# Layer normalisation, 16,384 rows of 1,024 floats: larger tiles in the in-place ring, new first tiles, and a second load queue at the start

## The chip, the cores and the metric

One core of one Trainium2 chip. The metric is the device time of one execution in microseconds (us), the median of several runs. The profile's span is about 2 us shorter than that time. All runs used here are at a granted clock of 1.0.

## The reference

```python
def reference(x, eps):            # x: (32, 512, 1024) float32
    mean = np.mean(x, axis=-1, keepdims=True)
    var = np.var(x, axis=-1, keepdims=True)
    return ((x - mean) / np.sqrt(var + eps)).astype(np.float32)
```

Each of 16,384 rows is normalised by itself. 67.1 MB are read, 67.1 MB written.

## The kernel before

A tile is K rows on each of the 128 partitions, K x 4 KB per partition. It is loaded into a ring of 48 rows per partition, normalised in place and stored from there. A slot is loaded again only after its store has landed.

```python
TILES = (2, 2, 4) + (8,) * 14 + (4, 2, 2)
RING = 48
GROUP = 8
# ...
    def rows_of(a, row, K):       # K rows of a partition lie together in HBM
        return a[row * P : (row + K) * P].rearrange("(p k) d -> p k d", p=P)
# ...
    def group(xs, G):              # its body in words
        # VectorE: 2 bn_stats per row (128x512 each)
        # GpSimd: nine small operations from the statistics to the sum of squares
        # ScalarE: sqrt; VectorE: reciprocal; GpSimd: -mean * rstd
        # ScalarE: one Identity activation per row, in place
# ...
        for K, row, pos in place(TILES, RING):
            nc.sync.dma_start(out=ring[:, pos : pos + K, :], in_=rows_of(x2, row, K))
            for g in range(0, K, GROUP):
                G = min(GROUP, K - g)
                group(ring[:, pos + g : pos + g + G, :], G)
            nc.scalar.dma_start(out=rows_of(o2, row, K), in_=ring[:, pos : pos + K, :])
```

## Time and profile before

| | before |
|---|---|
| time | 318.12 us (318.04 to 318.23, 3 runs) |
| span of the profiled run | 316.1 us |
| VectorE, ScalarE, GpSimd busy | 50%, 49%, 14% |
| load queue q1, store queue q10: share of the DMA engines' time | 49.6%, 49.3% |
| first packet, last packet ends | 1.76 us, 314.91 us |

The trace lists every DMA packet with start, duration and size. From that list I work out the *shortfall* at a time t: t less what the bytes moved by t would take at 435.2 GB/s (the ceiling that the prediction cites). It is the DMA time lost so far, averaged over the 16 engines, and it shows where it is lost.

### The profile page before, as it was taken

Reading aid. Unit: us, or ns where it says so; the run is one execution under the profiler, and the core shown is the slowest. Engines: PE = TensorE matmul, PEld = TensorE weight load, DVE = VectorE, ACT = ScalarE, POOL = GpSimd, SP = SyncE. Lnnn points to the kernel's source line nnn. Section 1 sums busy time; section 2 is a strip of 40 time slices with the busy share of each in tenths; the row PEclk is TensorE's granted clock in tenths of the full one; section 3 lists DMA queues with packets and bytes.
Section 4 is the critical chain, followed back from the end, with each engine's and each line's share of the span. In section 5 each row is a group of like instructions: output and inputs, shape, how many; then the busy total and the mean of one; then the engine's idle time right before and its main releaser. Section 6 shows DMA issues by size and latency. Waiting matters only on the chain.

```text
span 316.1 us, 794 instructions
## 1 busy us (share of the span) xinstructions
DVE 157.1 (50%) x277; ACT 154.3 (49%) x149; POOL 45.1 (14%) x204
## 2 busy tenths in 40 slices
DVE  2368596547092561916529074190652908363030
ACT  1336296692833809247091561900651956196321
POOL 0420202201102020020200202002020020221120
DMA  7999999999999999999999999999999999999996
GB/s 301 433 399 469 431 416 425 433 427 444 420 448 419 444 419 444 435 427 444 419 448 415 448 424 440 423 448 419 444 423 440 423 435 429 446 428 417 455 411 282
DMA packets 5766, 134.27 MB, mean 425 GB/s; under 512 B 640, under 2 KB 640, under 8 KB 640
## 3 DMA queue, kind: packets, MB, share of 16 engines
q1 hardware_dynamic: 2880, 67.11, 49.6%
q10 hardware_dynamic: 2880, 67.11, 49.3%
q14 instruction: 6, 0.05, 0.0%
HBM read 67.11 MB, written 67.11 MB: 425 GB/s over the span
## 4 chain that ended last, share of the span: by engine, by line
DMA 58%; DVE 17%; ACT 9%; POOL 6%; issue 3%; another core or an unknown queue 3%; ACTq 0%; POOLq 0%; DVEq 0%; SPq 0%
DMA ring<-in_x_dram 32%; DMA out_dram<-ring 27%; DVE stats L75 17%; ACT ring L111 8%; POOL half L64 1%; ACT std L103 1%; POOL dev L97 1%; POOL nmean L87 1%; POOL dev L100 1%; POOL dev L90 1%; POOL dev L96 1%; POOL nmean L67 1%; POOL ss L67 1%; DVE rstd L107 0%
## 5 line engine op out<-in xcount | busy, mean ns | idle before, releaser
L75 DVE BATCH_NORM_STATS2 stats<-ring 128x6 f32<-128x512 f32 x256 | 153.7, 678 | 71.2 <-DMA ring<-in_x_dram 71.2
L111 ACT ACTIVATE ring<-ring,nmr,rstd 128x1024 f32<-128x1024 f32 x128 | 147.0, 1227 | 10.8 <-POOL nmr L109 10.8
L103 ACT ACTIVATE std<-ss,eps_t 128x8 f32<-128x8 f32 (+2 forms) x20 | 6.0, 300 | 143.0 <-POOL ss L67 115.8
L107 DVE RECIPROCAL rstd<-std 128x8 f32<-128x8 f32 (+2 forms) x20 | 3.9, 193 | 77.3 <-ACT std L103 77.3
L64 POOL TENSOR_TENSOR half<-stats 128x16 f32<-128x16 f32 (+2 forms) x20 | 4.5, 226 | 221.0 <-DVE stats L75 221.0
L109 POOL TENSOR_TENSOR nmr<-nmean,rstd 128x8 f32<-128x8 f32 (+2 forms) x20 | 4.0, 202 | 27.2 <-DVE rstd L107 27.2
L97 POOL TENSOR_SCALAR dev<-dev 128x32 f32<-128x32 f32 (+2 forms) x20 | 5.6, 281 | 1.8
L100 POOL TENSOR_TENSOR dev<-dev,stats 128x32 f32<-128x32 f32 (+2 forms) x20 | 4.9, 243 | 1.7
L90 POOL TENSOR_TENSOR dev<-stats,nmean 128x32 f32<-128x32 f32 (+2 forms) x20 | 4.6, 231 | 1.7
L87 POOL TENSOR_SCALAR nmean<-nmean 128x8 f32<-128x8 f32 (+2 forms) x20 | 4.6, 228 | 1.8
L96 POOL TENSOR_TENSOR dev<-dev 128x32 f32<-128x32 f32 (+2 forms) x20 | 4.6, 228 | 1.6
L64 POOL TENSOR_TENSOR half<-dev 128x16 f32<-128x16 f32 (+2 forms) x20 | 4.2, 210 | 1.6
L67 POOL TENSOR_TENSOR nmean<-half 128x8 f32<-128x8 f32 (+2 forms) x20 | 4.0, 199 | 1.6
L67 POOL TENSOR_TENSOR ss<-half 128x8 f32<-128x8 f32 (+2 forms) x20 | 4.0, 199 | 1.6
L103 ACT ACT_TABLE_LOAD x1 | 1.3, 1283 | 0.9 <-DVE eps_t L120 0.9
L120 DVE MEMSET eps_t<- 128x1 f32 x1 | 0.1, 59 | 0.8 <-PEq L143 0.8
L143 POOL MEMSET const-float32-0.0<- 128x1 f32 x1 | 0.1, 98 | 0.2 <-issue 0.2
L143 POOL MEMSET const-uint8-127<- 128x1 uint8 x1 | 0.1, 102 | 0.0
L143 POOL MEMSET const-bfloat16-1.0<- 128x1 bf16 x1 | 0.1, 101 | 0.0
L143 POOL MEMSET const-float32-1.0<- 128x1 f32 x1 | 0.1, 98 | 0.0
## 6 DMA issues: line engine op xcount, KB each, us to landing
ring<-in_x_dram SPq DMA_DIRECT2D x14, 4096.0 KB, 47.3
out_dram<-ring ACTq DMA_DIRECT2D x14, 4096.0 KB, 40.7
ring<-in_x_dram SPq DMA_DIRECT2D x4, 1024.0 KB, 30.8
ring<-in_x_dram SPq DMA_DIRECT2D x2, 2048.0 KB, 27.2
out_dram<-ring ACTq DMA_DIRECT2D x4, 1024.0 KB, 16.7
out_dram<-ring ACTq DMA_DIRECT2D x2, 2048.0 KB, 24.5
```

What stands on the lines that cost most here:

```text
L64: nc.gpsimd.tensor_tensor(out=half[:, :G], in0=terms[:, :, 0:2], in1=terms[:, :, 2:4], op=ALU.add)
L67: nc.gpsimd.tensor_tensor(out=o, in0=half[:, :G, 0], in1=half[:, :G, 1], op=ALU.add)
L75: nc.vector.bn_stats(out=stats[:, k, s, :], in_=xs[:, k, s * BN_MAX : (s + 1) * BN_MAX],)
L87: nc.gpsimd.tensor_scalar(out=nmean[:, :G], in0=nmean[:, :G], scalar1=-1.0 / H, scalar2=None, op0=ALU.mult)
L90: nc.gpsimd.tensor_tensor(out=dev[:, :G], in0=mean4, in1=nmean[:, :G].unsqueeze(2).to_broadcast([P, G, H]), op=ALU.add,)
L96: nc.gpsimd.tensor_mul(out=dev[:, :G], in0=dev[:, :G], in1=dev[:, :G])
L97: nc.gpsimd.tensor_scalar(out=dev[:, :G], in0=dev[:, :G], scalar1=float(D // H), scalar2=None, op0=ALU.mult)
L100: nc.gpsimd.tensor_tensor(out=dev[:, :G], in0=dev[:, :G], in1=m2, op=ALU.add)
L103: nc.scalar.activation(out=std[:, :G], in_=ss[:, :G], func=AF.Sqrt, bias=eps_t, scale=1.0 / D)
L107: nc.vector.reciprocal(out=rstd[:, :G], in_=std[:, :G])
L109: nc.gpsimd.tensor_mul(out=nmr[:, :G], in0=nmean[:, :G], in1=rstd[:, :G])
L111: nc.scalar.activation(out=xs[:, k, :], in_=xs[:, k, :], func=AF.Identity, bias=nmr[:, k : k + 1], scale=rstd[:, k : k + 1],)
```

## The change

The intent is to move the same data in fewer, larger pieces: five slots of 10 rows for six of 8, a start with 6 and 4 rows on two queues, an end of 10 (computed as 6 and 4), 6 and 2. Small buffers come in pools of 3 and 10 for 4.

```diff
-TILES = (2, 2, 4) + (8,) * 14 + (4, 2, 2)
-RING = 48
-GROUP = 8
+TILES = (6, 4, 10, 10, 10, 10, 10, 10, 10, 10, 10, 10, 10, 6, 2)
+RING = 50
+GROUP = 10
+FINE = 6
+LAST = 3
 # ... pools: stats bufs 4 -> 3; the small tiles move to a pool with bufs=10 ...
 # ... place() becomes a loop that fills plan; load() holds the dma_start of a tile ...
-        for K, row, pos in place(TILES, RING):
-            nc.sync.dma_start(out=ring[:, pos : pos + K, :], in_=rows_of(x2, row, K))
-            for g in range(0, K, GROUP):
-                G = min(GROUP, K - g)
+        for t, (K, row, pos) in enumerate(plan[:2]):
+            load(nc.scalar if t == 1 else nc.sync, K, row, pos)
+        for t, (K, row, pos) in enumerate(plan):
+            if t > 1:
+                load(nc.sync, K, row, pos)
+            step = FINE if t >= len(TILES) - LAST else GROUP
+            for g in range(0, K, step):
+                G = min(step, K - g)
                 group(ring[:, pos + g : pos + g + G, :], G)
```

More of the change, by code (lines that the diff above doesn't have):

```diff
@@ L7 @@
 from concourse._compat import with_exitstack
-TILES = (2, 2, 4) + (8,) * 14 + (4, 2, 2)
-RING = 48
-GROUP = 8
-def place(tiles, ring):
-    plan, row, pos = [], 0, 0
-    for K in tiles:
-        if pos + K > ring:
-            pos = 0
-        plan.append((K, row, pos))
-        row += K
-        pos += K
-    return plan
+TILES = (6, 4, 10, 10, 10, 10, 10, 10, 10, 10, 10, 10, 10, 6, 2)
[3 more added lines that the diff above has]
+LAST = 3
 @with_exitstack
@@ L45 @@
     NSUB = D // BN_MAX
+    H = 2 * NSUB
     assert sum(TILES) * P == N
     rings = ctx.enter_context(tc.tile_pool(name="rings", bufs=1))
-    st = ctx.enter_context(tc.tile_pool(name="st", bufs=4))
+    st = ctx.enter_context(tc.tile_pool(name="st", bufs=3))
+    sm = ctx.enter_context(tc.tile_pool(name="sm", bufs=10))
     fdt = mybir.dt.float32
@@ L62, in pool_sum @@
         G = terms.shape[1]
-        half = st.tile([P, GROUP, 2], fdt, name="half")
+        half = sm.tile([P, GROUP, 2], fdt, name="half")
         nc.gpsimd.tensor_tensor(
@@ L78, in group @@
                 )
-        H = 2 * NSUB
         parts = stats[:, :G].rearrange("p g s (h c) -> p g (s h) c", h=2)
         mean4, m2 = parts[:, :, :, 1], parts[:, :, :, 2]
-        nmean = st.tile([P, GROUP], fdt, name="nmean")
-        dev = st.tile([P, GROUP, H], fdt, name="dev")
-        ss = st.tile([P, GROUP], fdt, name="ss")
+        nmean = sm.tile([P, GROUP], fdt, name="nmean")
+        dev = sm.tile([P, GROUP, H], fdt, name="dev")
+        ss = sm.tile([P, GROUP], fdt, name="ss")
         pool_sum(nmean[:, :G], mean4)
@@ L101, in group @@
         pool_sum(ss[:, :G], dev[:, :G])
-        std = st.tile([P, GROUP], fdt, name="std")
+        std = sm.tile([P, GROUP], fdt, name="std")
         nc.scalar.activation(
@@ L105, in group @@
         )
-        rstd = st.tile([P, GROUP], fdt, name="rstd")
+        rstd = sm.tile([P, GROUP], fdt, name="rstd")
         nc.vector.reciprocal(out=rstd[:, :G], in_=std[:, :G])
-        nmr = st.tile([P, GROUP], fdt, name="nmr")
+        nmr = sm.tile([P, GROUP], fdt, name="nmr")
         nc.gpsimd.tensor_mul(out=nmr[:, :G], in0=nmean[:, :G], in1=rstd[:, :G])
@@ L117, in group, with load @@
             )
+    def load(queue, K, row, pos):
+        queue.dma_start(out=ring[:, pos : pos + K, :], in_=rows_of(x2, row, K))
+    plan, row, pos = [], 0, 0
+    for K in TILES:
+        if pos + K > RING:
+            pos = 0
+        plan.append((K, row, pos))
+        row += K
+        pos += K
     with tc.manual_schedule():
         nc.vector.memset(eps_t, eps_val)
-        for K, row, pos in place(TILES, RING):
-            nc.sync.dma_start(out=ring[:, pos : pos + K, :], in_=rows_of(x2, row, K))
-            for g in range(0, K, GROUP):
-                G = min(GROUP, K - g)
+        for t, (K, row, pos) in enumerate(plan[:2]):
[6 more added lines that the diff above has]
+                G = min(step, K - g)
                 group(ring[:, pos + g : pos + g + G, :], G)
```

## The prediction

> **What bounds the kernel now.** I read the page's head and slices first, then its queue lines, then short windows at both ends, then the waits of the SyncE queue, and last the timeline of the final tiles.
>
> The head and the slices:
>
> ```profile
> span 316.1 us, 794 instructions
> DVE 157.1 (50%) x277; ACT 154.3 (49%) x149; POOL 45.1 (14%) x204
> ...
> DMA  7999999999999999999999999999999999999996
> ```
>
> No compute engine is busy for more than half of the span, and the DMA row is at 9 in every slice but the first and the last. The queue lines say how full that is:
>
> ```profile
> q1 hardware_dynamic: 2880, 67.11, 49.6%
> q10 hardware_dynamic: 2880, 67.11, 49.3%
> ...
> HBM read 67.11 MB, written 67.11 MB: 425 GB/s over the span
> ```
>
> The two queues (loads on q1, stores on q10) fill 49.6 + 49.3 = 98.9% of the 16 DMA engines' time. Only 1.1% of 316.1, 3.5 us, is idle in all. Windows at the two ends show where it is (columns: window, its length, DVE, ACT and POOL busy, clock, DMA share, GB/s):
>
> ```profile
> 1.50:2.00 0.50, 0.00 (x0) 0.50 (x1) 0.00 (x0) 1.00 0.30 33
> 2.00:2.50 0.50, 0.00 (x0) 0.21 (x1) 0.00 (x0) 1.00 0.52 164
> 2.50:3.00 0.50, 0.00 (x0) 0.00 (x0) 0.00 (x0) 1.00 0.76 311
> 3.00:3.50 0.50, 0.00 (x0) 0.00 (x0) 0.00 (x0) 1.00 0.97 410
> ```
>
> ```profile
> 310.00:313.00 3.00, 0.00 (x0) 0.00 (x0) 0.00 (x0) 1.00 1.00 423
> 313.00:314.00 1.00, 0.00 (x0) 0.00 (x0) 0.00 (x0) 1.00 0.53 221
> 314.00:315.00 1.00, 0.00 (x0) 0.00 (x0) 0.00 (x0) 1.00 0.10 41
> 315.00:316.10 1.10, 0.00 (x0) 0.00 (x0) 0.00 (x0) 1.00 0.00 0
> ```
>
> The first packet starts at 1.76 us and all 16 engines are at work by 3.0. The engines stop one by one between 313.2 and 314.9, and 1.2 us follow for the last landing and the end. The trace's packet records give an idle share of 2.4 us per engine before 4 us, 2.2 us after 313 us, and none between. So DMA throughput is the bound from end to end; the waits in the middle are only where the surplus shows:
>
> ```profile
> DVE stats L75 <- DMA ring<-in_x_dram: 71.2, 13, 7.3
> ACT std L103 <- DMA ring<-in_x_dram: 26.8, 2, 17.5
> ...
> SPq L122 <- DMA out_dram<-ring: 215.6, 12, 19.0
> ```
>
> SyncE waits 215.6 us for stores to land before it may refill a ring slot, and ACT once stood still 17.5 us on a load it does not even read (a landing semaphore that is used again). Neither left a hole in the DMA row, so the ring has slack.
>
> The end, from the timeline:
>
> ```profile
> 288.65 2.48 DVE L75 BATCH_NORM_STATS2 stats<-ring 128x6 f32<-128x512 f32 x4 [3.24 <-DMA ring<-in_x_dram]
> ...
> 300.78 2.47 DVE L75 BATCH_NORM_STATS2 stats<-ring 128x6 f32<-128x512 f32 x4 [6.54 <-DMA ring<-in_x_dram]
> ...
> 309.08 0.34 ACTq L126 DMA_DIRECT2D out_dram<-ring  x1
> ```
>
> The last load lands just before 300.78. From there to the issue of the last store are 8.3 us of compute, and the stores of older tiles cover them: the last store's first packets, at about 310.8, follow the previous store without a gap.
>
> **What the Trainium skill says.** "DMA: Bandwidth & Descriptors", section "Where 436 GB/s comes from", gives a ceiling of 16 ports at 435.2 GB/s, that is 27.2 bytes per ns and engine. The trace agrees: a 32,768-byte packet takes 1213 ns, 27.0 bytes per ns. Nothing can lift that rate. The same page, "Queues, rings and completion order", says that each DMA engine goes round robin between queues packet by packet. The trace agrees: the last two 2-row loads land 300.78 - 288.65 = 12.1 us apart, and 8 packets per engine at 0.309 (8 KB) + 1.213 us (the 32 KB store packets between them) make 12.2. Its section "Issuing engines are not separate DMA queues" says that a second issuing engine saves only sequencer time. The trace shows how little that is here: SyncE issues its first two loads at 0.72 and 1.14 us, and the first one's data keeps the engines busy from 1.76 to about 5 us.
>
> **The change, part by part.**
>
> *Bytes.* Unchanged: 67.11 MB each way. The DMA engines' 312.6 us (98.9% of 316.1) stay but for packets.
>
> *Larger tiles.* A partition's rows of one tile are one packet, and each of the 16 engines carries 8 partitions. The records show 309, 611 and 1213 ns for 2, 4 and 8 rows, which is bytes over 27.2 plus about 8.4 ns. So I estimate 912 ns for 6 rows and 1514 for 10. Before, one engine and one direction: 14 x 8 x 1213 + 2 x 8 x 611 + 4 x 8 x 309 + 20 semaphore writes x 9 ns = 155.7 us. After, with eleven tiles of 10 rows, two of 6, one of 4, one of 2: 88 x 1514 + 16 x 912 + 8 x 611 + 8 x 309 + 15 x 9 = 155.3 us. Both directions: 0.8 us less. It lies on the bound, so all of it counts: -0.8.
>
> *First loads of 6 and 4 rows on two queues.* Both go round robin with 8 packets per engine each, so they land together: 8 x (0.912 + 0.611) = 12.2 us after the start at some 2 to 2.6, about 15.3 us; the first statistics start there and not at 5.69. From there 12 statistics at 0.62 = 7.4, the small chain 3.4 (8.18 to 11.58 before), and 6 normalisations at 1.16 = 7.0: the first store goes out at about 33 us, not 13.99. That costs nothing by itself, since 50 rows of loads, 50 x 1.21 = 60 us of work, stand ready for the DMA meanwhile. What the second queue can win is part of the ramp between 1.76 and 3.0, which loses about 0.6 us of full rate: I take -0.2.
>
> *Five slots for six.* One tile's load and store then take 2 x 8 x 1.514 = 24.2 us, five of them 121 us per turn of the ring. A tile is in compute for about 20 x 0.6 + 3.4 + 10 x 1.16 = 27 us, perhaps 33 with waits (it was about 28 before: a turn of 6 x 19.4 = 116.5, less 47.3 and 40.7 us from issue to landing). So 88 us of the turn are left for two transfers that need 48 in mixed traffic: some 40 us, 1.7 tiles, always stand in the queues. Before it was 116.5 - 28.4 - 38.8 = 49 us, 2.5 tiles. Less slack, but more than none: 0.
>
> *Compute engines.* VectorE goes through a tile in 12 + 3.4 = 15.4 us, well inside 24.2. Fewer groups (16 for 20) take away some 40 GpSimd instructions, off the path: 0.
>
> *End, 10 (in groups of 6 and 4), 6, 2.* The load of 6 rows beside 40 KB store packets takes 8 x (0.912 + 1.514) = 19.4 us, that of 2 rows 8 x (0.309 + 1.514) = 14.6. Tile 12 has these 34 us for its some 24 of compute, so its store is ready about 10 us before the last load lands. Then up to 10 + 6 + 2 rows of stores, 22 us, remain against 14.6 before (300.3 to 314.9), and the last tile's 8.3 us of compute are covered. The end stays DMA, one 2-row store last: 0, with +0.3 as an allowance for a small hole.
>
> Sum: -0.8 - 0.2 + 0.3 = -0.7 us: 318.12 becomes about **317.4**.
>
> **Rivals.** (1) *A hole in mid-stream.* With five large slots, a load waits for the store of five tiles back, and a false wait on a reused semaphore, like the 17.5 us one of before, now lasts up to a tile pair of 24 us. Against it: two such waits left no hole before, and 1.7 tiles stand in the queues. If queues do run dry, each hole is some 3 us (first packet 1.0 us after issue, landing, restart): 319 to 322. I give it one in nine. (2) *The end is exposed.* If stores drain ahead of the last loads, the tail of 8.3 us plus about 1.5 us of issue shows in part; my count puts this at about 1 us: 318.5. (3) *The head wins more.* Were the reader to think of the first store's delay or of the second queue as the lever, it would be a gain of several us; the idle time to be had is 3.5 us in all, of which 1.76 lie before the first packet and 1.2 after the last. A gain cannot well be over 2 us: 316. (4) *40 KB packets are cut or slower.* If each is split, 88 x 8 ns more per direction turn the -0.8 into about +0.6: 318.7.
>
> **Range and chances.** Predicted 317.4 us; 8 in 10 between 316.2 and 319.1, the upper side longer because of the rivals 1, 2 and 4. Faster by over 2% would need 6.4 us, more than all idle time plus packet overhead: 0.01. Slower by over 2% needs two or more holes of rival 1: 0.03. Within 2%: 0.96.
>
> **What would show it.** Right: both queues together again at about 98.9% or 99%, 15 x 128 + 15 x 16 = 2160 packets for 2880 on each queue, 40 KB packets near 1514 ns, first statistics at about 15.3 us, first store at about 33, DMA row at 9 in all slices but the ends, and a span of about 315.4. Wrong: a slice of 8 or less in the middle (rival 1), a dip in the DMA share in the last 15 us (rival 2), packets of another size or rate (rival 4), or a ramp that ends much before 3.0 us (rival 3). If the time moved by more than 2 us without any of these, my reading of DMA as the only bound would be wrong.

## The result, and the profile after

The changed kernel takes 318.26 us (317.81 to 318.50, 4 runs), the kernel before 318.18 (318.04 to 318.56, 4 runs). The ratio is 0.9999, with a 95% interval of 0.9982 to 1.0016. Here and below a ratio is the mean time of one kernel's fast runs over the mean of the other's in the same rounds, so it is not quite the ratio of the medians quoted beside it. The change neither wins nor loses anything that can be measured.

The page of the changed kernel, its head, slices and queue lines:

```profile
span 316.6 us, 710 instructions
DVE 156.1 (49%) x273; ACT 152.6 (48%) x145; POOL 37.5 (12%) x164
...
DMA  8999999999999999999999999999999999999995
...
q10 hardware_dynamic: 2304, 69.21, 50.6%
q1 hardware_dynamic: 2016, 65.01, 48.1%
q14 instruction: 4, 0.03, 0.0%
```

The picture is that of before: 50.6 + 48.1 = 98.7% of the DMA time is taken, and no slice between the ends falls below 9. There are 4320 packets on the two queues for 5760. The one ScalarE load shows as 2.1 MB that moved from q1 to q10, and 144 packets with it; the prediction had overlooked this and said 2160 for each queue. The small queue q14 fetches instructions; it comes back below.

The start, from VectorE's timeline of the changed kernel:

```profile
16.11 7.21 DVE L68 BATCH_NORM_STATS2 stats<-ring 128x6 f32<-128x512 f32 x12 [15.26 <-DMA ring<-in_x_dram]
```

Statistics begin at 16.11 us for 5.69 before, and the first store goes out at 33.89 for 13.99. No time came of that delay of 20 us, since the DMA engines had loads to move. The windows in which the stores join the loads (columns as in the prediction), changed kernel:

```profile
30.00:35.00 5.00, 1.75 (x5) 4.16 (x5) 2.07 (x10) 1.00 0.99 426
35.00:40.00 5.00, 5.00 (x9) 4.63 (x4) 0.07 (x1) 1.00 0.99 333
40.00:45.00 5.00, 5.00 (x10) 0.00 (x0) 0.00 (x0) 1.00 0.95 411
```

The DMA share stays at 0.99, yet the rate drops to 333 GB/s for 5 us: the engines are busy with packets that take longer. (A packet counts in the window in which it starts, so windows this short are rough when packets last 1.5 us; the shortfall, which spreads each packet, gives the loss as 1.1 us. Between 16 and 60 us the packets took 1.15 us per DMA engine more than packets of their size take later; before, it was 0.72.) And the end, where the last store goes out on ScalarE's queue:

```profile
284.79 2.48 DVE L68 BATCH_NORM_STATS2 stats<-ring 128x6 f32<-128x512 f32 x4 [4.00 <-DMA ring<-in_x_dram]
...
293.09 0.34 ACTq L133 DMA_DIRECT2D out_dram<-ring  x1
```

```profile
312.00:313.00 1.00, 0.00 (x0) 0.00 (x0) 0.00 (x0) 1.00 0.93 393
313.00:314.00 1.00, 0.00 (x0) 0.00 (x0) 0.00 (x0) 1.00 0.61 254
314.00:315.00 1.00, 0.00 (x0) 0.00 (x0) 0.00 (x0) 1.00 0.08 33
```

The last store is issued at 293.09 us, 16 us earlier than before, and still the data runs out at the same time, because 22 us of stores, its own included, are still to be moved then. In the last row the share is 0.08: about one sixteenth. One DMA engine of the 16 works alone from 314.10 to 315.27, while the middle one stopped at 313.67.

The account of lost time, from the packet records (us; "middle" and "last" are the ends of the middle and the slowest DMA engine; the experiments' rows are explained below, the last column is the median time of all runs):

| kernel | shortfall at 30 | at 60 | at 300 | 60 to 300 | middle | last | time |
|---|---|---|---|---|---|---|---|
| before | 3.39 | 3.82 | 5.22 | 1.40 | 313.59 | 314.91 | 318.18 |
| changed | 2.85 | 4.18 | 5.28 | 1.10 | 313.67 | 315.27 | 318.26 |
| changed, repeated | 2.93 | 4.13 | 5.24 | 1.11 | 313.66 | 315.09 | 318.44 |
| before, 2nd load on ScalarE | 3.20 | 3.75 | 5.12 | 1.37 | 313.47 | 315.00 | 318.24 |
| changed, 2nd load on SyncE | 2.80 | 3.54 | 4.68 | 1.14 | 312.95 | 315.07 | 318.47 |
| changed, small head | 3.15 | 3.64 | 4.88 | 1.24 | 313.21 | 314.81 | 317.83 |
| the same, repeated | 3.18 | 3.58 | 4.83 | 1.25 | 313.06 | 314.97 | 317.84 |
| before, big head | 2.80 | 3.78 | 5.16 | 1.38 | 313.57 | 315.43 | 318.32 |
| changed, coarse end | 2.73 | 3.79 | 4.97 | 1.18 | 313.21 | 315.07 | 318.32 |
| before, 4 KB packets | 4.52 | 5.71 | 13.33 | 7.62 | 322.23 | 323.93 | 326.86 |
| changed, 1024 idle GpSimd instr. | 2.92 | 4.02 | 5.56 | 1.54 | 313.53 | 318.28 | 321.78 |

Three readings. In the steady stretch from 60 to 300 us the larger tiles save 0.3 us, and every kernel with 10-row tiles and no other dose (1.10 to 1.25) lies below every one with 8-row tiles (1.37 to 1.40). By 60 us the changed kernel has lost 0.3 to 0.4 us more than the one before, so the two cancel. And the end goes with the slowest DMA engine: in every row the span of the profiled run ends 1.2 to 1.4 us after "last", but 2.5 to 6.1 us after "middle". (The last column is a median over runs of which only one has a trace, so its differences of 0.2 us between rows say little.)

### The profile page after: what moved, and what is told of

Read it like the earlier page. It is cut to its first block, busy times and chain, and to the rows that moved or that the text cites. A ratio compares the mean times of both kernels' runs of the same rounds, so it can differ in the third digit from the quotient of the medians.

```text
span 316.6 us, 710 instructions
## 1 busy us (share of the span) xinstructions
DVE 156.1 (49%) x273; ACT 152.6 (48%) x145; POOL 37.5 (12%) x164
## 3 DMA queue, kind: packets, MB, share of 16 engines
q10 hardware_dynamic: 2304, 69.21, 50.6%
q1 hardware_dynamic: 2016, 65.01, 48.1%
## 4 chain that ended last, share of the span: by engine, by line
another core or an unknown queue 38%; DMA 32%; DVE 11%; ACT 7%; POOL 3%; issue 1%; SPq 1%; ACTq 0%; POOLq 0%; DVEq 0%
DMA ring<-in_x_dram 17%; DMA out_dram<-ring 15%; DVE stats L68 11%; ACT ring L103 7%; SPq L112 1%; POOL half L57 1%; ACT std L95 0%; POOL dev L89 0%; POOL dev L92 0%; POOL nmean L79 0%; POOL dev L82 0%; POOL dev L88 0%; POOL nmean L60 0%; POOL ss L60 0%
## 5 line engine op out<-in xcount | busy, mean ns | idle before, releaser
L95 ACT ACTIVATE std<-ss,eps_t 128x10 f32<-128x10 f32 (+3 forms) x16 | 4.8, 301 | 130.3 <-POOL ss L60 130.3
L57 POOL TENSOR_TENSOR half<-stats 128x20 f32<-128x20 f32 (+3 forms) x16 | 3.7, 233 | 231.8 <-DVE stats L68 231.8
L99 DVE RECIPROCAL rstd<-std 128x10 f32<-128x10 f32 (+3 forms) x16 | 3.3, 204 | 51.9 <-ACT std L95 51.9
L89 POOL TENSOR_SCALAR dev<-dev 128x40 f32<-128x40 f32 (+3 forms) x16 | 4.6, 289 | 1.4
L101 POOL TENSOR_TENSOR nmr<-nmean,rstd 128x10 f32<-128x10 f32 (+3 forms) x16 | 3.3, 205 | 10.6 <-DVE rstd L99 10.6
L92 POOL TENSOR_TENSOR dev<-dev,stats 128x40 f32<-128x40 f32 (+3 forms) x16 | 4.1, 259 | 1.3
L79 POOL TENSOR_SCALAR nmean<-nmean 128x10 f32<-128x10 f32 (+3 forms) x16 | 3.9, 244 | 1.4
L82 POOL TENSOR_TENSOR dev<-stats,nmean 128x40 f32<-128x40 f32 (+3 forms) x16 | 3.9, 245 | 1.3
L88 POOL TENSOR_TENSOR dev<-dev 128x40 f32<-128x40 f32 (+3 forms) x16 | 3.8, 239 | 1.3
L57 POOL TENSOR_TENSOR half<-dev 128x20 f32<-128x20 f32 (+3 forms) x16 | 3.4, 213 | 1.3
## 6 DMA issues: line engine op xcount, KB each, us to landing
ring<-in_x_dram ACTq DMA_DIRECT2D x1, 2048.0 KB, 15.6
```

Of the source, the lines that this page charges most:

```text
L57: nc.gpsimd.tensor_tensor(out=half[:, :G], in0=terms[:, :, 0:2], in1=terms[:, :, 2:4], op=ALU.add)
L79: nc.gpsimd.tensor_scalar(out=nmean[:, :G], in0=nmean[:, :G], scalar1=-1.0 / H, scalar2=None, op0=ALU.mult)
L82: nc.gpsimd.tensor_tensor(out=dev[:, :G], in0=mean4, in1=nmean[:, :G].unsqueeze(2).to_broadcast([P, G, H]), op=ALU.add,)
L88: nc.gpsimd.tensor_mul(out=dev[:, :G], in0=dev[:, :G], in1=dev[:, :G])
L89: nc.gpsimd.tensor_scalar(out=dev[:, :G], in0=dev[:, :G], scalar1=float(D // H), scalar2=None, op0=ALU.mult)
L92: nc.gpsimd.tensor_tensor(out=dev[:, :G], in0=dev[:, :G], in1=m2, op=ALU.add)
```

## The experiments

**My theory** after the result: both kernels are bound by the DMA engines; the larger tiles do save packet overhead, less than I said; a one-time loss where stores begin takes it back; and what is left is hidden by the slowest of the 16 engines. **Rivals**: the second queue costs what the tiles gain; the overhead of a packet is hidden, so that nothing could be gained; the shorter ring or the new end costs.

### Second load back on SyncE

```diff
-            load(nc.scalar if t == 1 else nc.sync, K, row, pos)
+            load(nc.sync, K, row, pos)
```

> The changed kernel with its second load back on SyncE's queue; nothing else differs. I call shortfall the time since the span's start less what the bytes moved so far would take at 435.2 GB/s; in the changed kernel it is 2.76 us at 10 us, in the kernel before 2.71. My theory: the second queue gains nothing, because the first packets' latency sets the ramp; shortfall at 10 us 2.6 to 2.9, first load of 6 rows lands near 10 us and not 16, time 318.2 within 0.5. Rival (the ScalarE load costs what the larger tiles gain, since the first packets took 1.2 to 2.7 us there): shortfall at 10 us 2.3 or less and 317.6 or less. Rival (it wins): 2.9 or more and 318.7 or more.

Measured: 318.47 us (317.94 to 318.87, 5 runs) for 318.02, ratio 1.0011 (0.9999 to 1.0023). Shortfall at 10 us 2.70 against 2.76 to 2.84. The first load now lands at 10.7 us, as VectorE's timeline shows, so the two queues had shared the bandwidth and nothing more:

```profile
10.73 7.21 DVE L68 BATCH_NORM_STATS2 stats<-ring 128x6 f32<-128x512 f32 x12 [9.88 <-DMA ring<-in_x_dram]
```

The start is the same with and without the second queue. There is a surprise later: the loss where stores begin was 0.6 us here and not 1.1, so the middle engine finished at 312.95, 0.7 earlier than in the changed kernel. The time did not follow. These windows at the end of this run show why:

```profile
310.00:313.00 3.00, 0.00 (x0) 0.00 (x0) 0.00 (x0) 1.00 0.84 355
313.00:314.00 1.00, 0.00 (x0) 0.00 (x0) 0.00 (x0) 1.00 0.14 57
314.00:315.00 1.00, 0.00 (x0) 0.00 (x0) 0.00 (x0) 1.00 0.06 25
```

A share of 0.06 is one engine of 16. Nearly all had stopped before 313.5, and one went on to 315.07.

### The kernel before with the second load on ScalarE

```diff
+        for t, (K, row, pos) in enumerate(place(TILES, RING)[:2]):
+            queue = nc.scalar if t == 1 else nc.sync
+            queue.dma_start(out=ring[:, pos : pos + K, :], in_=rows_of(x2, row, K))
-        for K, row, pos in place(TILES, RING):
-            nc.sync.dma_start(...)
+        for t, (K, row, pos) in enumerate(place(TILES, RING)):
+            if t > 1:
+                nc.sync.dma_start(...)
```

> The kernel before with this part of the change alone: its second load (2 rows) goes out on ScalarE's queue beside the first. My theory: no effect, ratio 0.999 to 1.001, shortfall at 10 us 2.6 to 2.8 against 2.71. Rival (the second queue costs at the start): shortfall 3.0 or more. Rival (it gains): 2.4 or less and 317.7 us.

Measured: 318.24 us (317.97 to 318.58, 5 runs) for 318.02, ratio 1.0009 (0.9996 to 1.0022); shortfall at 10 us 2.75. No effect, from the other side. The second queue neither gains nor costs.

### Small first tiles with 10-row tiles, twice

```diff
-TILES = (6, 4, 10, 10, ...
+TILES = (2, 2, 2, 4, 10, 10, ...
```

> The changed kernel with first tiles of 2, 2, 2 and 4 rows in place of 6 and 4. In the changed kernel the shortfall jumps from 2.87 us at 36 us to 4.02 at 41, when the first stores join the loads; before it rises from 2.75 at 16 us to 3.35 at 25. My theory: this one-time loss where stores begin, larger with large load packets under way, eats the saving of the larger tiles. With the first store near 15 us and small stores first, the loss should fall to 0.4 to 0.8 us in all, shortfall at 60 us 3.6 to 3.9 against 4.18, and the time to about 317.8. Rival (the loss belongs to 40 KB load packets whatever the head is): shortfall at 60 us 4.1 to 4.3 and 318.2 us.

> The kernel with the small head once more, as the candidate for the better version and to see whether its middle engine repeats at 313.2 and its last at 314.8: my theory says the middle does within 0.3 and the time is again within 0.3 us of before, since the last engine sets the end; a version that beats both clearly would need 0.997 or less, which I do not expect.

Measured: 317.83 us (5 runs of 6 between 317.60 and 317.86, one 319.15) for 318.02, ratio 0.9998 (0.9985 to 1.0011). The second time 317.84 (317.50 to 318.10) for 318.13, ratio 0.9987 (0.9972 to 1.0001). The shortfall at 60 us, 3.64 and 3.58, fell as my theory said, with 40 KB packets under way as in the changed kernel. This is the best version tried, some 0.2 to 0.3 us under before in the medians, which is inside the intervals. It does not clearly beat either kernel.

### Large first tiles with 8-row tiles

```diff
-TILES = (2, 2, 4) + (8,) * 14 + (4, 2, 2)
+TILES = (6, 4) + (8,) * 14 + (4, 2)
-RING = 48
+RING = 50
```

> The kernel before, 8-row tiles, with first tiles of 6 and 4 rows (the last ones 4 and 2, the ring 50 rows so that slots fit), both loads on SyncE. My theory: the loss where stores begin is set by the late, larger first stores meeting a full load queue: it grows from 0.6 to about 1 us here (shortfall at 60 us 4.1 to 4.3 against 3.82) and the time to about 318.6. Rival (the packet size of 40 KB makes the loss): shortfall at 60 us stays at 3.7 to 3.9 and 318.2 us.

Measured: 318.32 us (318.00 to 318.64, 5 runs) for 318.02, ratio 1.0008 (0.9996 to 1.0020). The loss from 30 to 41 us was 0.88 (2.80 to 3.68), in one step as I expected. But at 60 us the shortfall was 3.78, where I had said 4.1 to 4.3; the number speaks for the rival. With the small-head run, which speaks against it, neither simple rule holds. From 14 to 60 us the shortfall grew by 1.08 us before, 1.40 and 1.27 in the changed kernel's two traces, 0.81 with the load on SyncE, 0.81 and 0.65 with the small head, 1.06 here. That 0.6 to 1.4 us of DMA time are lost while the stores join is seen in every trace of the table but that with 4 KB packets. What sets its size is left open.

### Packets of 4 KB

```diff
-        return a[...].rearrange("(p k) d -> p k d", p=P)
+        return a[...].rearrange("(k p) d -> p k d", p=P)
```

> The kernel before with the rows of a tile dealt out so that a partition's rows lie apart in HBM: every packet is one row, 4096 bytes, and nothing else differs. It doses the term of my sum that should have gained 0.8 us. If each packet costs 8.4 ns on the path, a row takes 159 ns and not 152, 128 x 8 rows per engine and direction make 162.8 us for 155.7, both 14 us more: about 332 us. Rival (the cost per packet is hidden, so that larger packets cannot gain): 318 to 320 us. If the queue merges rows into larger packets, the packet count will say so.

Measured: 326.86 us (326.78 to 327.14, 4 runs) for 317.97, ratio 1.0276 (1.0260 to 1.0291). Its queue lines:

```profile
q1 hardware_dynamic: 16704, 67.11, 50.6%
q10 hardware_dynamic: 16704, 67.11, 50.2%
```

Each row is a packet now: 128 x 128 + 20 x 16 = 16,704. The edit also changes the order of the rows in HBM, but a packet takes 159 ns, as 4,096 bytes at 27.2 per ns plus 8.4 ns do, so that order did not slow them. The time per packet is on the path, so the rival that it is hidden falls. But it is smaller than I had read it. Both directions have 1728 packets more per engine, and the time rose by 8.89 us: 5.1 ns each, not 8.4. The two shares show the cause. They add up to 100.8%, more than there is: in the packet records a packet starts about 3 ns before the one ahead of it ends (one 8 KB store of the kernel before runs from 308.320 to 308.629 us, the next starts at 308.626), so durations taken from the records count the overlap twice. In the changed kernel this holds for 4303 of 4308 packets that follow another on the same engine: they start 3 or 4 ns early. The change saves 80 packets per engine in both directions together, 80 x 5.1 ns = 0.4 us, and 10 semaphore writes of 9 ns, 0.1 us. It could not save 0.8.

### A ring of four slots, and of three

```diff
-RING = 50
+RING = 40        # the other run: 30
```

> The changed kernel with four slots of 10 rows (ring of 40). My count of slack: a turn of the ring is then 4 x 24.2 = 97 us, less 27 to 33 of compute, less 48 of transfers: 15 to 20 us of slack, so the same time, 318 within 1. Rival (the ring of five is already short, and lost slack is where the gain went): slower by 2% or more, with DMA slices of 8 or less.

> The changed kernel with three slots of 10 rows (ring of 30). A turn at full rate is 72.6 us, and compute of 27 to 33 plus transfers of 48 plus some 6 of issue and landing need 81 to 87: the ring becomes the bound, 12 to 20% more in the stretch that turns, 350 to 375 us, with DMA slices well under 9. Rival (the loads and stores speed up when they are alone, so that a short ring costs little): under 330 us.

Measured: four slots 319.63 us (319.07 to 320.86, 4 runs) for 317.97, ratio 1.0056 (1.0027 to 1.0085). Three slots 337.37 us (336.12 to 337.79), ratio 1.0598 (1.0572 to 1.0623). The DMA row of the ring of three has holes in several places:

```profile
DMA  8999997999999998997999999997999999997997
GB/s 311 464 410 449 374 433 292 380 395 458 425 439 429 429 444 333 332 463 312 361 419 458 405 463 419 367 458 317 312 458 400 463 405 453 390 414 324 390 415 318
```

Both expectations missed. Four slots came out above my 318 within 1: they lose 1.3 us in one place (the shortfall goes from 3.58 at 60 us to 4.91 at 100), and the DMA engines are not idle there, the packets only last longer (1.25 us per engine between 60 and 300). Three slots lose 15.6 us in that stretch; longer packets make 8.6 us of it, most of it in steps of 0.6 to 1.1 us, and idle engines only about 6. I put the loss of three slots at 12 to 20%, and it was 6%. A likely reason is that I had counted every transfer at the mixed rate: for 132 of these 240 us one queue alone had over 90% of the engines' time. (Slices above 435 GB/s only show that a packet counts where it starts.) The trace of five slots has no such step, so the ring of the changed kernel has slack, and the gain did not go there.

### No taper at the end

```diff
-TILES = (6, 4, 10, ..., 10, 6, 2)
-FINE = 6
+TILES = (6, 4, 10, ..., 10, 8)
+FINE = 10
```

> The changed kernel without its taper: one last tile of 8 rows for 6 and 2, and no tile split in groups. In the changed kernel the last store goes out at 293.1 us and DMA works until 315.3, so 22 us of stores cover the end. With 8 rows the last load lands near 272.6, its compute takes about 22, the store goes out near 295 and still stands behind others: same time, 318.2 within 0.5. Rival (the end is exposed and the taper pays for something): 3 us or more slower.

Measured: 318.32 us (318.08 to 318.44, 4 runs) for 317.97, ratio 1.0005 (0.9990 to 1.0020). The last store goes out at 295.19 us for 293.09. The taper and the split into 6 and 4 pay for nothing here.

### The changed kernel once more

> The changed kernel once more, unchanged, to see how far a trace's numbers repeat: shortfall at 36, 41, 60, 300 us (2.87, 4.02, 4.18, 5.28 in the first trace) within 0.15 each, and the time the engines stop (315.27, one engine 1.2 us behind the others) anywhere between 314.3 and 315.5, which would make the straggler chance. If the shortfall at 41 us repeats as well, the loss where stores begin belongs to the kernel.

Measured: 318.44 us (318.19 to 319.18, 6 runs) for 318.12, ratio 1.0012 (0.9999 to 1.0025). The shortfalls at 36, 41, 60 and 300 us are 2.97, 3.98, 4.13 and 5.24; all repeat within 0.1. The last engine again stops alone, at 315.09 with the middle one at 313.66. So the trace's numbers can be trusted to about 0.1 us, and the loss where stores begin is not chance. By my own expectation 315.09 would still allow the straggler to be chance; the next runs settle that.

### Instructions that do nothing but be fetched

```diff
+        for _ in range(64):                       # before each group's normalisations
+            nc.gpsimd.memset(scratch, 0.0)        # the other run: 48 nc.vector.memset
```

> The changed kernel with 64 one-element memsets on GpSimd at the end of each group, 1024 in all: they do nothing but be fetched. In all traces so far one DMA engine stops near 315.0 us though the middle engine stops at 313.7 (changed), 313.6 (before) or 312.9 (changed, second load on SyncE), and an instruction fetch of 8 KB that lasts 0.31 us shows once per 128 instructions of an engine, 4 inside the span here. My theory: the fetches fall on few DMA engines, and the slowest engine, made late by them, sets the end; so 8 more fetches put the last engine 2.5 to 5 us later while the middle engine stays at 313.7 within 0.4: about 321 us. Rival (fetches are spread or harmless; the straggler has another cause): last engine within 0.6 of 315.2, 318.4 us.

> The same dose on VectorE: 48 one-element memsets after each group's reciprocal, 768 in all, 6 more fetches, some 3 us more per group on an engine with 24 us per tile for 15. My theory: last engine 1.9 to 4 us later, or, if each sequencer's fetches have a DMA engine of their own, another one becomes the straggler; the middle engine as before; 320 to 322 us. Rival: 318.4 within 0.6.

GpSimd, measured: 321.78 us (321.51 to 322.00, 5 runs) for 318.13, ratio 1.0111 (1.0096 to 1.0125). Its instruction queue and the windows at its end:

```profile
q14 instruction: 12, 0.10, 0.1%
```

```profile
313.00:314.00 1.00, 0.00 (x0) 0.00 (x0) 0.20 (x3) 1.00 0.49 205
314.00:315.00 1.00, 0.00 (x0) 0.00 (x0) 0.00 (x0) 1.00 0.23 98
315.00:316.00 1.00, 0.00 (x0) 0.00 (x0) 0.00 (x0) 1.00 0.08 33
316.00:317.00 1.00, 0.00 (x0) 0.00 (x0) 0.00 (x0) 1.00 0.08 33
317.00:318.00 1.00, 0.00 (x0) 0.00 (x0) 0.00 (x0) 1.00 0.08 33
```

Twelve fetches of 8 KB for four. The middle engine still stops at 313.53, and in the end one engine alone works on to 318.28, 3.0 us later than the last one of the changed kernel. The time rose by 3.3 to 3.5 us over the changed kernel's two medians. The rival, that fetches are harmless, falls.

Which engine serves which fetch stands in no view, but it can be worked out from the packet list. On one DMA engine a packet starts 3 or 4 ns before the one ahead of it ends, and each transfer gives each engine 8 packets and one semaphore write. Linked by these two rules, the packets of a trace fall into 16 chains of 8.389 MB each, one per engine. In the changed kernel the engine that ends at 315.27 carries two of the four fetches, those that end at 313.97 and 314.01 one each, the other 13 none. In the GpSimd run the engine that ends at 318.28 carries nine of the twelve. A fetch takes 0.31 us, and the packet behind it lasts 0.2 to 0.6 us longer than usual. For the last engine of the changed kernel that makes 2 x 0.31 + 0.53 + 0.56 = 1.7 us, and it stops 1.6 us after the middle one. In each of the first nine rows of the table the last engine is one that carries two fetches. (Fetches are not the only cause of delay: one engine without any stopped at 316.48 in the GpSimd run, and why is open.)

Together with the run on SyncE, this shows from both sides what sets the end: there the middle engine gained 0.7 us and the time nothing; here the middle engine lost nothing and the time 3.4 us.

VectorE, measured: 323.23 us (323.14 to 323.68, 4 runs), ratio 1.0160 (1.0144 to 1.0177). The time alone does not test the fetches, for another thing happened. The memsets took some 6 us per group where I had said 3, and at the end, where four groups follow one another, the next-to-last store went out at 308.95 for 288.02:

```profile
295.00:300.00 5.00, 3.39 (x6) 0.00 (x0) 1.12 (x6) 1.00 0.98 419
300.00:305.00 5.00, 1.73 (x28) 3.28 (x4) 1.11 (x5) 1.00 0.72 311
305.00:310.00 5.00, 3.63 (x25) 3.92 (x4) 0.00 (x0) 1.00 0.23 98
```

The stores in hand ran out and the shortfall grew by 5.2 us between 300 and 310. All engines then stopped together at 319.7, none behind. The chains show the fetches all the same: eight of the ten lie on one engine, which works through without a pause, while each of the other 15 stands idle for 4.2 to 6.2 us up to 309.8 and so lets it catch up. Eight is 2 + 6, and nine in the GpSimd run is 1 + 8, as if each compute engine's fetches went through one DMA engine. The time came out 1 us above my range by a mechanism I had not named. It does show how far the end is covered: a delay of 21 us at the last stores was hidden but for 5.

## Why the prediction was right, and where its sum was not

**Same time, within the range: right.** 318.26 us lies between 316.2 and 319.1. The reason given, DMA bound from end to end with only a few us of idle time, held: 98.7% after, and neither the queue, nor the first tiles, nor the end moved the time by 0.2% when undone or done alone. Its idle time was read 1.1 us too low, though: 3.5 us from the shares, while the same paragraph has 2.4 + 2.2 = 4.6 us at the two ends. The overlap of packets, counted twice in the shares, makes the difference (some 360 packets per engine x 3.3 ns = 1.2 us).

**The mean came out 0.9 us too low** (317.4 against 318.26), through these terms:

- *Larger tiles, -0.8.* The mechanism was right, the size was not. The term is the cost of a packet: 8.4 ns read from durations, 5.1 ns as the 4 KB run measures it. The saving is about 0.5 us in all; 0.3 of it is seen between 60 and 300 us. The estimates of the packets themselves held: 40 KB took 1514 ns at the least, 24 KB 912.
- *Second queue, -0.2.* Wrong: 0 in time, from both sides. Two queues have the first packets of both loads in flight, and these simply last longer: the shortfall at 10 us is the same 2.7 to 2.8.
- *First tiles: 0.* The times were right within an us (16.11 for 15.3, 33.89 for 33), and the delay of the first store is hidden. Missing was that the stores, when they join, slow the loads that are under way. In both kernels that costs about 1 us, in the changed one some 0.3 more. Nothing in my reading looked at the rate inside the DMA row's nines.
- *Five slots: 0.* Right for five. The count of slack behind it was too kind: it left 15 to 20 us for four slots, and these cost 0.6%.
- *The end, +0.3 for a small hole.* No hole came, since the last store waits behind 22 us of others. I was right on the cover, and the late engines were there in the profile before, as a share of 0.10 from 314 to 315. I took them for the way engines stop one by one, and did not see that the latest one, not the mean of the 16, sets the time, nor that it is one with two fetches (of six, before).

**Rivals.** (1) no hole in mid-stream, and no wait of ScalarE for a load: right to give it little. (2) not exposed. (3) a gain of over 2 us: none. (4) 40 KB packets are whole and at full rate: 1514 ns, 27.1 bytes per ns.

**Where the expected gain went**, then: 0.3 of 0.8 was never there, and about 0.3 to 0.4 went into the dearer start of the stores. So the middle engine stopped at 313.67 for 313.59: in the changed kernel itself nothing was left to hide. Where a run did gain 0.4 to 0.7 us at the middle engine (load on SyncE, small head, coarse end), the time did not follow, or by at most 0.4, since one engine finished 1.6 to 2.1 us after it. Shown is that this engine sets the end and that the fetches it carries delay it, by about 0.85 us each in the changed kernel. What sets the size of the loss where stores begin stays open. That the result came out so near to no change is partly luck: the saving in packets and the loss at the stores, which I had not foreseen, are about equal.

## What to carry to other kernels

When two DMA queues add up to 99% of the engines' time, more queues and tapered ends have nothing to win, and bigger tiles only what packets cost (5.1 ns each here; 2.8% with 4 KB packets); check the idle share before the waits, since 215 us of waits on one queue cost nothing here. Measure a per-item cost by a dose (eight times the packets) rather than from recorded durations, because pipelined items overlap. And at the end of a DMA-bound kernel look at the last window's share: one sixteenth means that a single engine sets the time, and fewer instructions, not fewer packets, may be what helps it. No run here tries fewer instructions alone.

## What the Trainium skill lacked or had wrong

- "DMA: Bandwidth & Descriptors", section "Specifications", gives some 0.6 us to the first byte on the sync and scalar path. It does not say from where this counts. Here the first packet starts 1.04 us (before) and 1.01 us (changed) after the issue begins; the first issue itself takes 0.37 us, so that is 0.64 to 0.67 us after its end. The ramp to full rate adds about 1.0 us of shortfall, which the section leaves out.
- The same page, "Queues, rings and completion order", tells of the round robin but not of its price when a second direction joins: some 0.6 to 1.4 us of DMA time, once, with the DMA share at 0.99 and the rate at 333 GB/s.
- "Runtime: NRT & Kernel Launch", section "Instruction fetch mechanics", says that instructions are refilled in 16 KiB blocks of 256 and that the cost is mostly hidden. In these traces the fetches are 8 KB, 0.31 us, one per about 128 instructions of an engine (8 more for 1024 memsets), and they are not hidden in a kernel bound by DMA: an engine with two ended 1.6 us after the middle one, one with nine 4.75 us. No page gives such a cost.
- No page says that the recorded durations of consecutive packets on one DMA engine overlap, by 3 to 4 ns here: the shares of the 4 KB run add up to 100.8%, and the cost of a packet is 5.1 ns for the 8.4 that the durations give.
